# First stage of a two-mixer transformer layer: modulation weights loaded first, x second, two tiles of h modulated from PSUM

## The chip, the cores and the metric

The kernel runs on one core of one Trainium2 chip, in one launch. The metric is device time in microseconds (us) of that launch, taken as the median of several runs; the kernel before was run three times for the numbers below. All data are float32; matmuls that have to be fast take float32 operands split into a high and a low part.

## The reference

x has 2048 rows (tokens) of 1024 columns, c is one vector of 1024. The layer is a modulated token mixer with two kinds of attention, followed by a gated MLP with a short convolution, and a last normalization:

```python
mod = jax.nn.silu(c) @ w_ada[l] + b_ada[l]
shift_a, scale_a, gate_a, shift_m, scale_m, gate_m = [
    m[:, None, :] for m in jnp.split(mod, N_MOD, axis=-1)]

h = rms_norm(x, g_attn[l]) * (1.0 + scale_a) + shift_a
proj = h @ w_in[l]
q_f, k_f, v_f, q_s, k_s, v_s, f_logit = jnp.split(proj, offsets, axis=-1)
...
x = x + gate_a * (mix @ w_out[l])

h = rms_norm(x, g_mlp[l]) * (1.0 + scale_m) + shift_m
...
return rms_norm(x, g_final)
```

Only the first three statements matter here, and of these only the first block of 512 tokens, and the q and k of the first pair of heads of the second attention ("sb", stick-breaking).

## The kernel before

**Tiling.** The tokens are cut into four blocks of 512 (TB), each loaded as four tiles of 128 tokens by 1024 columns. h is kept turned: eight tiles (kt = 0 to 7) of 128 columns by 512 tokens. A unit of attention is a pair of heads of one kind over one block; the first unit is ("sb", 0, 0), and the stage before it is `first_block` (L479).

**What the stage makes.** It needs the columns shift_a and 1 + scale_a (times the gain g_attn) as `mod_a`, 128 partitions by 2 by 8. They come from the first 2048 columns of w_ada, 1024 rows, in four groups g of 256 columns of shift and 256 of scale; group g serves the tiles kt = 2g and 2g + 1. `load_ada(g)` (L173) loads a group with eight DMAs, one for each tile k of 128 rows of w_ada. The class `mod_cols` (L255) sums a group over the 1024 rows in two ways. `add` multiplies row tiles by silu(c) and sums them on DVE (VectorE, L265 and L267) into one tile; DIRECT (L252) says how many of the eight row tiles go this way. `total` (L269) does the rest on PE (TensorE, L275): for each remaining row tile, and once for DVE's partial sum (`None` in the list), four matmuls with a moving operand of a single column. Each float32 matmul shows as two instructions in the profile. `finish` (L277) adds the terms out of the PSUM bank on DVE and puts bias and gain in (L281 to L285).

**What keeps PE at work.** `keep_warm(n)` (L475) issues n matmuls of 256 columns on constants, into a bank that nobody reads. WARM (L251) gives two such numbers and FILL (L252) is the number after every total (L519).

**The rest of the stage.** `normalize_block` (L164) squares and sums a tile of x on ACT (ScalarE, L100), takes the root (L101), the reciprocal on DVE (L102), and scales the tile on DVE (L168). A turn of tile kt is four transposes on PE into one bank (L494); ACT copies the bank to SBUF as `stage` (L495). `stage_h(kt)` (L499) modulates on ACT (L501), splits the result into a high part (ACT, L45) and a low part (DVE, L46), and stores both to DRAM for later units (SP's queue, L505). `project_h(kt)` (L508) is six matmuls (L342), three each for q and k, with the split weights `w[0]`; `w[1](kt)` splits one tile of these weights (L45, L46). `unpack_rows` (L244) turns the small parameter rows (gains, bias) into columns.

**Order.** All loads go out on SP's queue in the order of L215 to L242: c, block 0 of x, the small rows, group 0 of w_ada, half of the raw q and k weights, group 1, the other half, groups 2 and 3, the v weights, block 1 of x. A planner orders the instructions of each engine, from a timeline of its own, except where `fixed()` (L206) ties them: what is traced inside such a block follows, on its engine, whatever the blocks before it issued there. `do(fn, ...)` (L512) is such a block around one call, so that the first stage's order on PE, ACT and DVE is the order of the calls written out. PSUM banks come from pools: `pt` has three, used both by the turns and by the sums of `mod_cols`.

The order of calls before: eight warm-up calls; all four tiles of x normalized; the rows turned and three warm-up calls; all eight turns with their copies; then group 0 is added and totalled, and in a loop over g the sums of group g + 1 are run between the modulations and projections of group g.

Of the kernel before, what the change touches and what calls it, by code (L numbers as in the profile page):

```python
# [9 lines left out]
F32 = mybir.dt.float32  # L10
# [7 lines left out]
P = 128  # L18
# [16 lines left out]
def kernel(ctx: ExitStack, tc: tile.TileContext, x, c, w_ada, b_ada, g_attn, w_in, b_fgate,  # L35
# [125 lines left out]
    def begin_block(tb):  # L161
        blocks.append(load_x(tb))
# [42 lines left out]
    @contextmanager  # L205
    def fixed():  # L206
        with ExitStack() as order:
            for ins in last.values():
                order.enter_context(tc.issue_after(ins))
            n = len(nc.cur_bb.bb.instructions)  # L210
            yield
        for ins in nc.cur_bb.bb.instructions[n:]:
            last[ins.engine] = ins
# [6 lines left out]
        nc.scalar.activation(cs, b[:, :KT], AF.Silu)  # L220
    NR = R_BA + 6 * KT
    rows = sm.tile([NR, P], F32, name="rows")
    begin_block(0)
    for r, src in ((R_GA, g_attn), (R_GM, g_mlp), (R_GF, g_out_fox), (R_GS, g_out_sb), (R_BA, b_ada)):
        n = src.shape[1] // P
        nc.sync.dma_start(rows[r:r + n], src[0].rearrange("(t p) -> t p", p=P))
    load_ada(0)
    raw_qk = load_raw(3 * 512, 4)
    raws = {"qk": next(raw_qk)}
    load_ada(1)  # L230
# [18 lines left out]

    warm = pj()  # L250
    WARM = (8, 3)  # L251
    DIRECT, FILL = 6, 1  # L252
    SPLIT = 4

    class mod_cols:  # L255
# [222 lines left out]

    def first_block(w):  # L479
        xts = blocks[0]  # L480
        with fixed():
            keep_warm(WARM[0])
        for i, xt in enumerate(xts):
            with fixed():
                normalize_block([xt])
        with fixed():
            unpack_rows()
            keep_warm(WARM[1])
        stage = [sb.tile([P, 2, TB], F32, name="xT", tag="K", bufs=5) for _ in range(KT // 2)]
        for kt in range(KT):  # L490
            b = pt()
            with fixed():
                for i, xt in enumerate(xts):
                    nc.tensor.transpose(b[:, i * P:(i + 1) * P], xt[:, kt * P:(kt + 1) * P], ident)  # L494
                nc.scalar.activation(stage[kt // 2][:, kt % 2], b, AF.Copy)  # L495
        aq, ak = pj(), qk()
        hts = []

        def stage_h(kt):  # L499
            hf = px.tile([P, TB], F32, name="hf_a", bufs=2)  # L500
            nc.scalar.activation(hf, stage[kt // 2][:, kt % 2], AF.Identity, scale=mod_a[:, 0, kt:kt + 1],  # L501
                                 bias=mod_a[:, 1, kt:kt + 1])
            h = h_tile()
            split(h[:, 0], h[:, 1], hf, nc.vector)
            nc.sync.dma_start(hs[0][kt], f(h))  # L505
            hts.append(h)

        def project_h(kt):  # L508
            accumulate(aq, 0, w[0], hts[kt], kt)
            accumulate(ak, 1, w[0], hts[kt], kt)  # L510

        def do(fn, *args):  # L512
            with fixed():
# [4 lines left out]
                do(m.total, k)  # L518
                do(keep_warm, FILL)  # L519

        ms = [mod_cols(g) for g in range(KT // 2)] + [None]
        do(ms[0].add, 0, DIRECT)
        do(w[1], 0)
        do(w[1], 1)
        total(ms[0], *range(DIRECT, KT - 1), None, KT - 1)
        for g in range(KT // 2):
            m = ms[g + 1]
            if m:
                do(m.add, 0, 3)
            do(ms[g].finish)  # L530
            if m:
                total(m, *range(DIRECT, KT - 1))
            do(stage_h, 2 * g)
            do(project_h, 2 * g)
            if m:
                do(m.add, 3, DIRECT)
            do(stage_h, 2 * g + 1)
            if m:
                do(w[1], 2 * g + 2)
                do(w[1], 2 * g + 3)  # L540
                total(m, None, KT - 1)
            do(project_h, 2 * g + 1)
        
        with fixed():
            w[1:] = [w[2]()]
        with fixed():
# [1216 lines left out]
```

## Time and profile before

| what | value |
|---|---|
| median of 3 runs | 2947.29 us (2942.23 to 2953.07) |
| the profiled run's own time | 2943.39 us |
| its span on the core | 2941.4 us, 45922 instructions |
| mean granted TensorE clock in it | 0.993 of full speed |
| DMA | 601.89 MB, mean 205 GB/s |

The profile is of one execution. Engines: PE is TensorE's matmuls, PEld its weight loads, DVE VectorE, ACT ScalarE, POOL GpSimd, SP the engine that issues DMAs. A row of the timeline gives start, duration (both us), engine, line, operation, output<-inputs, shapes, how many instructions were merged (x), and in brackets how long the engine was idle before it and what ended that. In a row of a wait, three numbers give the total of us, the times, and the longest. Line 13 of the kernel is L13. A busy PE is not PE at its peak, for the clock that it is granted varies; the views of windows give it as a share of full speed.

### The profile page before, as it was taken

The page shows a single profiled execution, that of the slowest core. Times are in us where ns is not written, and L with a number is a line of the kernel's source. Part 1 is how long each engine was busy: PE and PEld are TensorE (multiplying, and loading weights), DVE is VectorE, ACT ScalarE, POOL GpSimd, SP SyncE. Part 2 cuts the span into 40 slices and gives each one's busy share as a digit, 9 for nine tenths or more (in the row PEclk, how much of TensorE's full clock was granted, in tenths as well). Part 3 has the DMA queues.
Part 4 walks back from the last instruction along what each step waited for, and adds up shares of the span by engine and source line. Part 5 has one row for each costly group of instructions (what it writes and reads, how often), then busy time and mean ns, then how long its engine had stood idle before and what let it go on. Part 6 is the DMA issues. An engine that isn't in the chain of part 4 may idle for free.

```text
span 2941.4 us, 45922 instructions
## 1 busy us (share of the span) xinstructions
PE 2867.8 (97%) x15772; PEld 2459.7 (84%) x15772; DVE 2179.5 (74%) x3464; ACT 1686.0 (57%) x3187; POOL 901.1 (31%) x967
## 2 busy tenths in 40 slices
PE   8999999999999999999999999999999999999998
PEld 7888888888988988888888788888788888888887
DVE  5787778877886656658843788888998888575476
ACT  5776767677776656658744554444444445433342
POOL 0431322243032423231213344444254543142200
PEclk8999999999999999999999999999999999999999
DMA  9749756867469794794537775554754444975644
GB/s 293 255 139 321 236 188 207 301 211 229 162 212 356 269 277 139 232 323 140 182 120 233 245 232 128 130 136 129 236 132 125 130 130 132 309 257 185 216 158 151
DMA packets 348346, 601.89 MB, mean 205 GB/s; under 512 B 34672, under 2 KB 178800, under 8 KB 348112
## 3 DMA queue, kind: packets, MB, share of 16 engines
q1 hardware_dynamic: 324208, 558.06, 57.7%
q0 software_dynamic: 10880, 20.97, 4.3%
q10 hardware_dynamic: 13024, 19.93, 1.9%
q8 instruction: 124, 2.03, 0.3%
q14 instruction: 110, 0.90, 0.1%
HBM read 420.77 MB, written 177.02 MB: 203 GB/s over the span
## 4 chain that ended last, share of the span: by engine, by line
PE 46%; DMA 3%; DVE 2%; SPq 1%; ACT 1%; issue 1%; POOL 0%; DVEq 0%; ACTq 0%; POOLq 0%
PE ps_o L1315 19%; PE ps_t L1315 7%; PE ps_o L1614 6%; PE ps_t L1614 3%; PE ps_bc L1614 3%; PE ps_o L912 1%; PE ps_pv L615 1%; DMA r<-rstd 1%; PE ps_bc L912 1%; PE ps_pt L606 1%; PE ps_o L1609 1%; DMA wo<-wos 1%; DMA hm<-hf_m 1%; SPq L895 1%; DVE op L46 1%
## 5 line engine op out<-in xcount | busy, mean ns | idle before, releaser
L1315 PE MATMUL ps_o<-op,wu 128*128 128x512 f32 x2592 | 608.0, 389 | 2.0 <-DVE snap L1366 1.5
L1315 PEld LDWEIGHTS ps_o<-op,wu 128*128 128x128 f32 x2592 | 486.2, 188 | 103.9 <-DVE snap L1366 1.9
L611 DVE TENSOR_TENSOR at<-ps_pt,at 128x512 fp32r<-128x512 f32 (+1 forms) x576 | 366.1, 652 | 100.2 <-ACT at L610 97.3
L636 DVE TENSOR_TENSOR_SCAN a<-r,a 128x512 f32<-128x512 f32 (+2 forms) x320 | 368.3, 1167 | 77.8 <-ACT a L631 39.9
L342 PE MATMUL ps_pj<-hp,w_qk 128*128 128x512 f32 x1512 | 411.2, 403 | 14.5 <-DMA hp<-hs 12.9
L610 ACT ACTIVATE at<-ps_pt 128x512 fp32r<-128x512 f32 (+1 forms) x576 | 318.5, 576 | 139.1 <-PE ps_pt L606 123.1
L615 PE MATMUL ps_pv<-at,V 128*128 128x256 f32 x2216 | 386.8, 292 | 9.3 <-DVE at L611 4.2
L615 PEld LDWEIGHTS ps_pv<-at,V 128*128 128x128 f32 x2216 | 320.9, 190 | 39.8 <-DVE at L611 11.4
L342 PEld LDWEIGHTS ps_pj<-hp,w_qk 128*128 128x128 f32 x1512 | 275.4, 190 | 71.0 <-DMA hp<-hs 16.2
L45 ACT ACTIVATE wu<-wuraw 128x512 fp32r<-128x512 f32 x204 | 128.9, 632 | 248.5 <-PE ps_o L1315 190.1
L596 PE MATMUL ps_qk<-K,Q 128*128 128x512 f32 (+2 forms) x640 | 265.7, 416 | 5.6 <-ACT a L631 3.3
L413 PE MATMUL ps_pj<-w_v,hp 128*128 128x256 f32 (+1 forms) x1536 | 236.6, 288 | 2.1 <-DVE hp L422 1.6
L597 PE MATMUL ps_qk<-K,Q 128*128 128x512 f32 (+2 forms) x640 | 235.7, 369 | 0.0
L1315 PE MATMUL ps_t<-op,wu 128*128 128x512 f32 x888 | 220.8, 390 | 1.0 <-DVE op L46 1.0
L413 PEld LDWEIGHTS ps_pj<-w_v,hp 128*128 128x128 f32 x1536 | 209.0, 189 | 10.9 <-DVE q L373 1.5
L630 ACT ACTIVATE r<-ps_qk 128x512 f32<-128x512 f32 (+2 forms) x320 | 173.1, 541 | 58.2 <-PE ps_qk L597 55.5
L46 DVE TENSOR_TENSOR wu<-wuraw,wu 128x512 fp32r<-128x512 f32 x204 | 189.6, 930 | 18.1 <-ACT wu L45 16.7
L1315 PEld LDWEIGHTS ps_t<-op,wu 128*128 128x128 f32 x888 | 166.4, 188 | 36.5 <-DVE op L46 1.8
L606 PE MATMUL ps_pt<-edge,a 128*128 128x128 f32 x1088 | 185.1, 274 | 8.4 <-DVE a L636 7.8
L1614 PE MATMUL ps_o<-op 128*128 128x512 f32 x840 | 191.5, 389 | 0.0
L1614 PEld LDWEIGHTS ps_o<-op 128*128 128x128 f32 x840 | 157.7, 188 | 32.7
L679 ACT ACTIVATE p<-p,mn 128x128 f32<-128x128 f32 (+15 forms) x128 | 153.9, 1203 | 53.3 <-DVE mn L675 52.2
(342 smaller groups left out, 5237.6 us busy)
## 6 DMA issues: line engine op xcount, KB each, us to landing
hp<-hs SPq DMA_DIRECT2D x224, 512.0 KB
wuraw<-in_w_up_dram SPq DMA_DIRECT2D x80, 512.0 KB
ra<-g SPq DMA_DIRECT2D x136, 256.0 KB
rb<-in_w_down_dram SPq DMA_DIRECT2D x108, 256.0 KB
g<-u SPq DMA_DIRECT2D x80, 256.0 KB
hs<-hp SPq DMA_DIRECT2D x32, 512.0 KB
hp<-in_w_ada_dram SPq DMA_DIRECT2D x32, 512.0 KB
qk_fox<-q SPq DMA_DIRECT2D x32, 512.0 KB
```

Source lines behind the costliest of these rows:

```text
L46: (lo_engine or nc.gpsimd).tensor_sub(lo, src, f(hi))
L342: nc.tensor.matmul(acc, w[kt][:, a, n], h[:, bb], start=kt == 0 and i == 0, stop=kt == KT - 1 and i == 2)
L413: nc.tensor.matmul(av[:, t * width:(t + 1) * width], hts[kt][:, a, tok], w[1][kt][:, bb, 0:width], start=kt == 0 and m == 0, stop=kt == KT ...
L596: nc.tensor.matmul(b[:, :cw], Q[:, hl, 0, qcols], K[:, hl, :cw], start=True, stop=False)
L597: marks.append(nc.tensor.matmul(b[:, :cw], Q[:, hl, 1, qcols], K[:, hl, :cw], start=False, stop=True).ins)
L606: nc.tensor.transpose(b[:, i * P:(i + 1) * P], blk(kts[kk], qi), ident)
L610: copies = [nc.scalar.activation(at[:, 0, lo:], b[:, lo:], AF.Copy).ins, nc.vector.tensor_sub(at[:, 1, lo:], b[:, lo:], f(at[:, 0, lo:])).ins]
L611: nc.vector.tensor_sub(at[:, 1, lo:], b[:, lo:], f(at[:, 0, lo:])).ins]
L615: m = nc.tensor.matmul(o[:, 0:2 * P], V[kt // 4][:, kt % 4, hl, :], rhs, start=first and kk == 0 and w == 0, stop=last and kk == 1 and w == 1)
L636: nc.vector.tensor_tensor_scan(rev, r[:, 0:need][:, ::-1], rev, 0.0 if right[qi] is None else right[qi][:, 0:1], ALU.mult, ALU.add)
L1315: nc.tensor.matmul(b, w[:, p, j], o[:, q], start=first and i == 0, stop=last and i == 2, skip_group_check=True)
L1614: nc.tensor.matmul(b, a[:, p, t * P:(t + 1) * P], w[:, q], start=first and i == 0, stop=last and i == 2, skip_group_check=True)
```

## The change

The edit moves and reorders work; what is computed stays the same.

- Loads: the eight DMAs of group 0 of w_ada go out ahead of block 0 of x on SP's queue. The five small loads of rows go out on ACT's queue instead of SP's.
- DIRECT is 4 instead of 6, so that each group has five totals on PE (row tiles 4, 5, 6, DVE's partial sum, row tile 7) instead of three, each followed by its warm-up call, and two additions fewer on DVE.
- Group 0 of the modulation is summed and finished ahead of the normalization of x. Three warm-up calls follow each of the four tiles of x, where three calls stood once.
- The tiles kt = 0 and 1 are modulated by ACT straight from the bank into which they are turned. The other six turns and copies are moved into the loop: tiles 2 and 3 ahead of the first projection, tiles 4 to 7 behind the second.
- The sums of group 1 follow those turns; the sums of groups 2 and 3 are spread as before, with the additions cut 2 and 2.

```diff
     NR = R_BA + 6 * KT
     rows = sm.tile([NR, P], F32, name="rows")
-    begin_block(0)
     for r, src in ((R_GA, g_attn), (R_GM, g_mlp), (R_GF, g_out_fox), (R_GS, g_out_sb), (R_BA, b_ada)):
         n = src.shape[1] // P
-        nc.sync.dma_start(rows[r:r + n], src[0].rearrange("(t p) -> t p", p=P))
+        nc.scalar.dma_start(rows[r:r + n], src[0].rearrange("(t p) -> t p", p=P))
     load_ada(0)
+    begin_block(0)
...
-    DIRECT, FILL = 6, 1
+    DIRECT, FILL = 4, 1
...
 
     def first_block(w):
         xts = blocks[0]
-        with fixed():
-            keep_warm(WARM[0])
-        for i, xt in enumerate(xts):
-            with fixed():
-                normalize_block([xt])
-        with fixed():
-            unpack_rows()
-            keep_warm(WARM[1])
-        stage = [sb.tile([P, 2, TB], F32, name="xT", tag="K", bufs=5) for _ in range(KT // 2)]
-        for kt in range(KT):
-            b = pt()
-            with fixed():
-                for i, xt in enumerate(xts):
-                    nc.tensor.transpose(b[:, i * P:(i + 1) * P], xt[:, kt * P:(kt + 1) * P], ident)
-                nc.scalar.activation(stage[kt // 2][:, kt % 2], b, AF.Copy)
+        stage = {}
         aq, ak = pj(), qk()
         hts = []
-
-        def stage_h(kt):
-            hf = px.tile([P, TB], F32, name="hf_a", bufs=2)
-            nc.scalar.activation(hf, stage[kt // 2][:, kt % 2], AF.Identity, scale=mod_a[:, 0, kt:kt + 1],
-                                 bias=mod_a[:, 1, kt:kt + 1])
-            h = h_tile()
-            split(h[:, 0], h[:, 1], hf, nc.vector)
-            nc.sync.dma_start(hs[0][kt], f(h))
-            hts.append(h)
-
-        def project_h(kt):
-            accumulate(aq, 0, w[0], hts[kt], kt)
-            accumulate(ak, 1, w[0], hts[kt], kt)
 
         def do(fn, *args):
             with fixed():
...
                 do(m.total, k)
                 do(keep_warm, FILL)
 
-        ms = [mod_cols(g) for g in range(KT // 2)] + [None]
-        do(ms[0].add, 0, DIRECT)
+        def turn(kt):
+            b = pt()
+            for i, xt in enumerate(xts):
+                nc.tensor.transpose(b[:, i * P:(i + 1) * P], xt[:, kt * P:(kt + 1) * P], ident)
+            return b
+
+        def stage_x(kt):
+            if kt % 2 == 0:
+                stage[kt // 2] = sb.tile([P, 2, TB], F32, name="xT", tag="K", bufs=5)
+            nc.scalar.activation(stage[kt // 2][:, kt % 2], turn(kt), AF.Copy)
+
+        def modulated(kt, src):
+            hf = px.tile([P, TB], F32, name="hf_a", bufs=2)
+            nc.scalar.activation(hf, src, AF.Identity, scale=mod_a[:, 0, kt:kt + 1], bias=mod_a[:, 1, kt:kt + 1])
+            h = h_tile()
+            hts.append(h)
+            nc.scalar.activation(h[:, 0], hf, AF.Copy)
+            return hf, h
+
+        def low(kt, hf, h):
+            nc.vector.tensor_sub(h[:, 1], hf, f(h[:, 0]))
+            nc.sync.dma_start(hs[0][kt], f(h))
+
+        def project_h(kt):
+            accumulate(aq, 0, w[0], hts[kt], kt)
+            accumulate(ak, 1, w[0], hts[kt], kt)
+
+        direct = range(DIRECT, KT - 1)
+        do(keep_warm, WARM[0])
+        m = mod_cols(0)
+        do(m.add, 0, DIRECT)
+        do(unpack_rows)
+        total(m, *direct, None, KT - 1)
+        do(m.finish)
+        for xt in xts:
+            do(normalize_block, [xt])
+            do(keep_warm, WARM[1])
         do(w[1], 0)
         do(w[1], 1)
-        total(ms[0], *range(DIRECT, KT - 1), None, KT - 1)
+        first = []
+        with fixed():
+            first.append(modulated(0, turn(0)))
+            first.append(modulated(1, turn(1)))
         for g in range(KT // 2):
-            m = ms[g + 1]
-            if m:
-                do(m.add, 0, 3)
-            do(ms[g].finish)
-            if m:
-                total(m, *range(DIRECT, KT - 1))
-            do(stage_h, 2 * g)
+            n = mod_cols(g + 1) if g + 1 < KT // 2 else None
+            a = first[0] if g == 0 else None
+            if g:
+                do(m.finish)
+                with fixed():
+                    a = modulated(2 * g, stage[g][:, 0])
+            if n and g:
+                do(n.add, 0, 2)
+            do(low, 2 * g, *a)
+            if g == 0:
+                do(stage_x, 2)
+                do(stage_x, 3)
+            elif n:
+                total(n, *direct)
             do(project_h, 2 * g)
-            if m:
-                do(m.add, 3, DIRECT)
-            do(stage_h, 2 * g + 1)
-            if m:
+            if n and g:
+                do(n.add, 2, DIRECT)
+            if g:
+                with fixed():
+                    a = modulated(2 * g + 1, stage[g][:, 1])
+            else:
+                a = first[1]
+            do(low, 2 * g + 1, *a)
+            if n:
+                if g == 0:
+                    do(n.add, 0, DIRECT)
                 do(w[1], 2 * g + 2)
                 do(w[1], 2 * g + 3)
-                total(m, None, KT - 1)
-            do(project_h, 2 * g + 1)
-        
+                if g == 0:
+                    do(project_h, 1)
+                    for kt in range(4, KT):
+                        do(stage_x, kt)
+                    total(n, *direct)
+                total(n, None, KT - 1)
+            if g:
+                do(project_h, 2 * g + 1)
+            m = n
+
         with fixed():
             w[1:] = [w[2]()]
         with fixed():
```

## The prediction, made before the run

> **What bounds the kernel now.** I read the page first, then the first stage in windows, what ACT waits for there, and TensorE's own timeline. Over the whole run TensorE is the engine that sets the pace:
>
> ```profile
> PE 2867.8 (97%) x15772; PEld 2459.7 (84%) x15772; DVE 2179.5 (74%) x3464; ACT 1686.0 (57%) x3187; POOL 901.1 (31%) x967
> ```
>
> The change touches only the stage before attention, so I look at it in stretches of 20 us (columns: start:end, length, then busy time and instructions of PE, PEld, DVE, ACT, POOL, then the granted clock, DMA share, GB/s):
>
> ```profile
> 20.00:40.00 20.00, 18.10 (x76) 15.66 (x75) 13.04 (x29) 6.78 (x12) 0.00 (x0) 0.66 1.10 338
> ...
> 60.00:80.00 20.00, 18.22 (x131) 16.05 (x130) 13.47 (x22) 14.18 (x33) 5.96 (x8) 1.00 0.81 247
> 80.00:100.00 20.00, 17.43 (x105) 15.07 (x104) 16.83 (x22) 13.60 (x28) 11.27 (x9) 1.00 0.98 336
> ACT hf_a L501 <- DVE mod_a L285: 20.6, 4, 8.3
> ```
>
> From 20 to 40 us PE is busy 18.10 of 20, but its clock is 0.66 of full speed. The last row, of the view of waits, says that ACT stands 20.6 us in total for mod_a, the modulation columns. The timeline tells who makes mod_a late:
>
> ```profile
> 2.51 7.00 PE L477 MATMUL ps_pj<-edge,ones 128*128 128x256 f32 x22
> 10.45 0.25 PE L246 MATMUL ps_pv<-edge,rows 72*128 72x72 f32 x1 [0.93 <-ACT at L100]
> ...
> 13.00 5.05 PE L494 MATMUL ps_pt<-edge,xt 128*128 128x128 f32 x29 [1.04 <-DVE xt L168]
> 18.77 0.68 PE L477 MATMUL ps_pj<-edge,ones 128*128 128x256 f32 x2
> 19.29 0.95 PE L275 MATMUL ps_pt<-ones,adas 128*128 128x1 f32 x8
> ...
> 20.61 0.95 PE L275 MATMUL ps_pt<-cs,ada 128*128 128x1 f32 x8
> 21.42 0.68 PE L477 MATMUL ps_pj<-edge,ones 128*128 128x256 f32 x2
> 24.00 1.84 PE L275 MATMUL ps_pt<-cs,ada 128*128 128x1 f32 x8 [1.90 <-ACT hp L45]
> ...
> 26.34 0.99 PE L342 MATMUL ps_pj<-hp,w_qk 128*128 128x512 f32 x1
> ...
> 29.26 1.70 PE L275 MATMUL ps_pt<-ones,adas 128*128 128x1 f32 x8
> ...
> 31.82 1.71 PE L275 MATMUL ps_pt<-cs,ada 128*128 128x1 f32 x8
> ...
> 38.25 0.58 PE L342 MATMUL ps_pj<-hp,w_qk 128*128 128x512 f32 x1
> ...
> 39.83 0.95 PE L275 MATMUL ps_pt<-ones,adas 128*128 128x1 f32 x8
> ...
> 54.72 0.62 PE L342 MATMUL ps_qk<-hp,w_qk 128*128 128x512 f32 x2
> ```
>
> The reader is to see a PE that works almost without a gap from 24.0 us to the end of the stage at 54.72 + 0.62 = 55.3 us, at two speeds. One row of w_ada summed on PE with its one warm-up call ("a total") takes 20.61 - 19.29 = 1.32 us in the fast part and 31.82 - 29.26 = 2.56 in the slow one; the six matmuls of one projection take 39.83 - 38.25 = 1.58 against 29.26 - 26.34 = 2.92. One warm-up call is two instructions of the first row: 2 x 7.00/22 = 0.64 us. The clock in fine windows of PE alone (length, busy, clock, DMA, GB/s):
>
> ```profile
> 13.20:13.60 0.40, 0.40 (x5) 0.74 0.96 318
> 16.80:17.20 0.40, 0.40 (x5) 0.99 1.17 327
> 23.60:24.00 0.40, 0.00 (x0) 0.54 1.19 309
> 37.20:37.60 0.40, 0.40 (x5) 0.89 1.09 348
> 20.23:23.64 3.41, 1.87 (x13) 1.00 1.10 345
> 1642.12:1645.53 3.41, 1.55 (x7) 1.00 0.98 358
> ```
>
> The clock falls at 13.4, rises at 16.8, falls at 23.6 and rises at 37.3: distances of 3.4, 6.8 and 13.7 us, multiples of one step of 3.41. It spends 13.7 us at half speed after PE ran out of work from 22.1 to 24.0. That loss, about 13.7/2 = 6.8 us of PE work, and the gap of 1.9, is what an order without gaps could win back here.
>
> **The change, part by part.** The times at which one group of mod_a is used, and what the loads and normalization cost:
>
> ```profile
> 22.49 0.81 ACT L501 ACTIVATE hf_a<-xT,mod_a 128x512 f32<-128x512 f32 x1 [3.10 <-DVE mod_a L285]
> 23.87 0.80 ACT L501 ACTIVATE hf_a<-xT,mod_a 128x512 f32<-128x512 f32 x1
> 34.23 0.81 ACT L501 ACTIVATE hf_a<-xT,mod_a 128x512 f32<-128x512 f32 x1 [8.28 <-DVE mod_a L285]
> 42.81 0.81 ACT L501 ACTIVATE hf_a<-xT,mod_a 128x512 f32<-128x512 f32 x1 [5.13 <-DVE mod_a L285]
> 50.39 0.82 ACT L501 ACTIVATE hf_a<-xT,mod_a 128x512 f32<-128x512 f32 x1 [4.12 <-DVE mod_a L285]
> 5.10 1.06 ACT L100 ACTIVATE at<-xt 128x1024 f32<-128x1024 f32 x1 [2.30 <-DMA xt<-in_x_dram]
> 12.19 0.75 DVE L168 TENSOR_SCALAR xt<-xt,ss_a 128x1024 f32<-128x1024 f32 x1
> 13.71 3.90 DVE L267 SCALAR_TENSOR_TENSOR adas<-ada,cs,adas 128x512 f32<-128x512 f32 x5
> 3.10 0.62 SPq L226 DMA_DIRECT2D rows<-in_g_attn_dram  x1
> ...
> 5.09 0.32 SPq L226 DMA_DIRECT2D rows<-in_b_ada_dram  x1
> ada<-in_w_ada_dram SPq DMA_DIRECT2D x32, 256.0 KB
> ```
>
> (a) *Loads.* Eight DMAs of 256 KB, 2.1 MB, now go ahead of x. At the 338 GB/s of the stretch from 20 to 40 us that is 6.2 us, so the last tile of x, scaled at 12.19 + 0.75 = 12.9 us before, is scaled at 19.1. The first 0.5 MB of x was there at 5.10; the first two weight rows now take that place, and the other six follow by 5.1 + 1.57/0.338 = 9.7, early enough for the sums below. The total of bytes ahead of the later groups is the same, so they land when they did. The five small loads of rows leave SP's queue for ACT's, where nothing else is to be done before x arrives; PE needs them at 7.6 us. SP spent 5.09 + 0.32 - 3.10 = 2.3 us on issuing them, while the DMA engines were at work on x, so leaving SP gains nothing that the path sees. Bounds: 0, to +2.3 us should they reach PE late by that much; I take 0. The eight stores of h are issued as before, one per tile, and nothing in this stage reads them.
>
> (b) *PE's opening.* Everything here is in a fixed order: 8 warm-up calls, 2.51 + 8 x 0.64 = 7.6; the turning of rows, 0.25 in the quoted row, 7.9; five totals (rows 4, 5, 6, the partial sum of DVE, row 7, for DIRECT is 4), 5 x 1.32 = 6.6, 14.5; then three warm-up calls after each of the four tiles of x, 12 x 0.64 = 7.6, which wait for nothing: 22.1. Only then comes the first turn of x. On DVE the end of group 0's sums now stands ahead of the scaling of x: it waits for PE's last total, which starts at 7.9 + 4 x 1.32 = 13.2, and is through at 13.2 + 1.88 = 15.1 (the 1.88 is worked out in d); the four scalings behind it, 0.75 and a small reciprocal each, end near 19.1 as well. So x, ready at 19.1, is covered by 3.0 us of warm-up; that cover hides the later x entirely. Were the calls gone, the turn would start at 19.1.
>
> (c) *The two direct tiles.* The next rows price a turn (four transposes), a copy out of the bank, and a modulation that reads a bank, as L569 does:
>
> ```profile
> 70.49 1.47 PE L564 MATMUL ps_pt<-edge,xt 128*128 128x128 f32 x12
> 15.72 0.60 ACT L495 ACTIVATE xT<-ps_pt 128x512 f32<-128x512 f32 x1 [0.25 <-PE ps_pt L494]
> 68.53 1.45 ACT L569 ACTIVATE xm<-ps_pt,mod_a 128x512 f32<-128x512 f32 x2 [5.69 <-PE ps_pt L564]
> 69.94 0.36 PE L596 MATMUL ps_qk<-K,Q 128*128 128x256 f32 x1 [0.74 <-DMA K<-q]
> ```
>
> A turn is 4 x 1.47/12 = 0.5 us. The modulation from a bank, 1.45/2 = 0.73, costs what it does from SBUF (0.81). So the first modulation starts at 22.1 + 0.5 + 0.1 = 22.7, against 22.49: no gain, 0.2 lost. Two copies of 0.60 go from ACT, off the path.
>
> (d) *What is late next.* Six turns that before lay ahead of 18 us now stand behind the first modulation. Turns 2 and 3 need the banks of the first two tiles, the second read until 22.7 + 1.38 + 0.80 = 24.9 (1.38 is 23.87 - 22.49): a new wait in PE's queue, and the first projection stands behind it. Turn 3 ends at 25.5, two projections at 28.7, four turns at the pace of ACT's copies (0.60) about 31.0. Then the sums of group 1: five totals instead of three. The last starts at 31.0 + 4 x 1.32 = 36.3; from the start of the last total to the modulation took 22.49 - 20.61 = 1.88, so group 1 is modulated at 38.2, 3.9 us later than 34.23, and PE is free at 37.6.
>
> (e) *Groups 2 and 3.* Per group PE now does 5 x 1.32 + 2 x 1.58 = 9.8 us. DVE gives up two additions of 3.90/5 = 0.78 per group, and was not the engine that ended the waits. PE: three totals 41.6, projection 43.1, last total starts 44.4, group 2 modulated 46.3 (42.81 before), PE free 45.8; projection 47.4, three totals 51.3, projection 52.9, last total starts 54.2, group 3 modulated at 56.1 against 50.39. From there the two last projections ended 55.3 - 50.39 = 4.9 us later, so the stage ends at 61.0.
>
> *Sum:* 61.0 - 55.3 = +5.7 us. Taken apart: eight more totals (20 instead of 12, 10.6) and nine more warm-up calls (20 instead of 11, 5.8) in PE's stream, less the half-speed loss (6.8); the remaining 3.9 is gaps that the denser stream closes, 1.9 of them the one from 22.1. Behind the stage PE has work waiting in order, busy 18.22 of the 20 us from 60, so I carry the 5.7 through whole. The profiled run took 2943.4 us (a span of 2941.4 and 2.0 around it): 2949.1. The median of the three runs shown lies 3.9 above that run, so the forecast for a median is 2953.0.
>
> *The clock, weighed.* The sum needs full speed through stretches that hold only totals, where warm-up fills 0.68 of every 1.32 us, 51%. No such window was seen at full speed. Bounds from the quoted windows: 20.23:23.64 was followed by a fall though it was busy 1.87 of 3.41; but only some 1.2 us of that, 36%, were warm-up calls, the rest matmuls of a single column, so I read it that these do not count. 1642.12:1645.53, busy 1.55 (45%) with wide matmuls, was followed by no fall. The 51% lie above the kept window, so I take "holds" at no cost; "falls" is the second case. The Trainium skill, "TensorE: Matmul & The Clock Gate", Part 1, has the clock halved only after an idle window of about 3.4 us; here 1.9 us of idleness sufficed, so the trace disagrees, and the second case below keeps its chance. Its Part 4 says that transposes do not count as busy to that gate; by that rule the stretch from 22.1 to 25.5 would count as idle and cost one more half-speed stretch, 6.8 us, to 2959.8, which the second case takes in. The trace disagrees again: transposes alone (L494) filled 13.4 to 16.8, and the clock rose at the end.
>
> **The rivals.** *Half clock (slower).* In the stretch of totals from 31.0 to 41.6 the clock falls and, as from 23.6 to 37.3, a lone projection does not raise it. For it: totals and short projections stayed at half for 13.7 us before. Against it: 45% was enough elsewhere. Price: between one more such stretch, +6.8, and all of 37.6 to 61.0 at half, +23.4; with the 5.7, 2960 to 2976, taken at 2966. It decides where the share of warm-up in a window falls below what keeps the gate open.
>
> *Absorbed (not slower).* The first attention matmul waited for K at 69.94, and PE is idle 20 - 18.22 = 1.8 and 20 - 17.43 = 2.6 us in the two stretches to 100 us. If these waits are on transfers that a later first stage does not delay, 4.4 of the 5.7 are taken up: +1.3, 2948.6. Against it: PE was busy 18.22 of 20 us around K's arrival, with work that a later stage shifts whole.
>
> *Order elsewhere.* Only the first stage's order is fixed; the rest is planned anew around it. PE's idle time, 2941.4 - 2867.8 = 73.6 us, could shift by a third, 25 us, either way: 2928 or 2978. Nothing in the profile speaks for a sign.
>
> **How the numbers follow.** Forecast 0.48 (its own range 2949 to 2959: up by the 2.3 us of (a) and by two steps at half speed, 3.4; down by the 3.9 between profiled run and median), half clock 0.27, absorbed 0.15, order 0.10. The range runs from 2940 to 2974, which leaves out the ends of the second and fourth case. About 0.5%, 14.7 us, is what a measurement of this kernel can tell from no change. Slower by more: 0.23 of half clock, 0.05 of order, 0.02 of the forecast, 0.30. Faster by more: 0.05 of order, 0.02 of absorbed, 0.07. Within: 0.63.
>
> **What would show it.** Right: twelve warm-up calls between the last total of group 0 and the first turn, no PE gap before 22 us, modulations near 22.7, 38, 46 and 56 us, the last projection ending near 61, and a clock of 1.0 from 17 to 61. Wrong: a half clock in the totals (second rival); the first turn waiting for x beyond 22 us, which would mean that the loads cost more than (a); totals below 1.3 us; or an end of the stage near 61 with attention's first matmul still at 70 (third).

## The result, and the profile after

The changed kernel took 2967.88 us (median of five runs, 2965.64 to 2979.19) against 2948.97 us before: a ratio of 1.0074, 95% interval 1.0059 to 1.0088. It is slower by more than the 0.5% that a measurement of this kernel can tell. The profiled execution took 2967.88 us with a span of 2966.2, 24.8 us longer than the span of before, 2941.4. The execution of before that was profiled took 2943.39 us, 5.6 below its median, so the two profiles lie further apart than the two medians (18.9 us).

The busy times of the whole run (the first part of the page), and then the first stage in stretches of 20 us (start:end, length, busy time and instructions of PE, PEld, DVE, ACT, POOL, then the granted clock, DMA share and GB/s), of the changed kernel:

```profile
PE 2887.4 (97%) x15870; PEld 2477.5 (84%) x15870; DVE 2172.4 (73%) x3456; ACT 1686.0 (57%) x3185; POOL 902.5 (30%) x967
```

```profile
20.00:40.00 20.00, 19.15 (x117) 16.96 (x116) 10.34 (x22) 9.61 (x19) 0.00 (x0) 0.87 1.09 336
40.00:60.00 20.00, 19.69 (x108) 17.02 (x107) 6.82 (x19) 5.54 (x9) 0.00 (x0) 0.87 0.86 287
60.00:80.00 20.00, 18.13 (x136) 16.99 (x136) 11.62 (x35) 13.57 (x38) 0.17 (x1) 1.00 0.56 159
```

PE is busy 19.6 us more than before (2867.8) and idle 5.2 more: 2966.2 - 2887.4 = 78.8 against 73.6. From 20 to 60 us it hardly stands still, as the prediction wanted, but its clock is 0.87, not 1.00. The same stage on PE's timeline (start, length, then the instructions; the wait before a row in brackets):

```profile
2.74 6.05 PE L477 MATMUL ps_pj<-edge,ones 128*128 128x256 f32 x16
...
14.04 0.95 PE L275 MATMUL ps_pt<-cs,ada 128*128 128x1 f32 x8
14.85 5.86 PE L477 MATMUL ps_pj<-edge,ones 128*128 128x256 f32 x26
20.55 1.47 PE L497 MATMUL ps_pt<-edge,xt 128*128 128x128 f32 x12
22.35 0.66 PE L497 MATMUL ps_pt<-edge,xt 128*128 128x128 f32 x4 [0.32 <-ACT hf_a L507]
23.53 0.50 PE L342 MATMUL ps_pj<-hp,w_qk 128*128 128x512 f32 x1 [0.53 <-ACT hp L510]
...
28.45 1.05 PE L275 MATMUL ps_pt<-cs,ada 128*128 128x1 f32 x8
29.36 0.68 PE L477 MATMUL ps_pj<-edge,ones 128*128 128x256 f32 x2
29.88 0.95 PE L275 MATMUL ps_pt<-cs,ada 128*128 128x1 f32 x8
...
33.85 0.95 PE L275 MATMUL ps_pt<-cs,ada 128*128 128x1 f32 x8
34.66 1.08 PE L477 MATMUL ps_pj<-edge,ones 128*128 128x256 f32 x2
35.53 1.71 PE L275 MATMUL ps_pt<-cs,ada 128*128 128x1 f32 x8
...
38.09 1.71 PE L275 MATMUL ps_pt<-cs,ada 128*128 128x1 f32 x8
...
62.16 0.62 PE L342 MATMUL ps_qk<-hp,w_qk 128*128 128x512 f32 x2
```

From 28.45 us there is nothing on PE but totals; at about 34.7 their matmuls go from 0.95 to 1.71 us, and a total from 1.32 to 38.09 - 35.53 = 2.56. The stage ends at 62.16 + 0.62 = 62.8 us, against 55.3 before and 61.0 in the forecast. The clock around that point, in windows of PE alone (length, busy, clock, DMA, GB/s), and the modulations on ACT:

```profile
31.07:34.48 3.41, 3.41 (x29) 1.00 1.10 349
...
34.50:34.90 0.40, 0.40 (x4) 0.88 1.10 348
34.66:45.00 10.34, 10.34 (x39) 0.51 0.85 257
...
45.00:45.40 0.40, 0.40 (x3) 0.95 1.07 440
```

```profile
12.61 1.06 ACT L100 ACTIVATE at<-xt 128x1024 f32<-128x1024 f32 x1 [9.40 <-DMA xt<-in_x_dram]
...
21.52 1.45 ACT L507 ACTIVATE hf_a<-ps_pt,mod_a 128x512 f32<-128x512 f32 x2 [1.44 <-PE ps_pt L497]
...
35.57 0.81 ACT L507 ACTIVATE hf_a<-xT,mod_a 128x512 f32<-128x512 f32 x1 [6.20 <-DVE mod_a L285]
...
48.43 0.82 ACT L507 ACTIVATE hf_a<-xT,mod_a 128x512 f32<-128x512 f32 x1 [9.40 <-DVE mod_a L285]
...
57.83 0.81 ACT L507 ACTIVATE hf_a<-xT,mod_a 128x512 f32<-128x512 f32 x1 [5.94 <-DVE mod_a L285]
```

PE was busy 3.41 of the 3.41 us before the fall, so idleness did not drop the clock. It stayed at half for 10.24 us, three steps of 3.41. Group 0 is modulated 1.0 us sooner than before (22.49), group 1 1.3 us later (34.23), groups 2 and 3 by 5.6 and 7.4 (42.81, 50.39): the part at half speed lies between.

### The profile page after: what moved, and what is told of

The parts are those of the page before. It is cut to its first block, busy times and chain, and to the rows that moved or that the text cites. A ratio compares the mean times of both kernels' runs of the same rounds, so it can differ in the third digit from the quotient of the medians.

```text
span 2966.2 us, 46096 instructions
## 1 busy us (share of the span) xinstructions
PE 2887.4 (97%) x15870; PEld 2477.5 (84%) x15870; DVE 2172.4 (73%) x3456; ACT 1686.0 (57%) x3185; POOL 902.5 (30%) x967
## 4 chain that ended last, share of the span: by engine, by line
PE 45%; DMA 2%; DVE 2%; SPq 1%; issue 0%; ACT 0%; POOL 0%; DVEq 0%; ACTq 0%; POOLq 0%
PE ps_o L1347 19%; PE ps_t L1347 7%; PE ps_o L1646 6%; PE ps_t L1646 3%; PE ps_bc L1646 3%; PE ps_o L944 2%; PE ps_bc L944 1%; DMA r<-rstd 1%; PE ps_o L1641 1%; SPq L927 0%; PE ps_pv L647 0%; DMA hm<-hf_m 0%; PE ps_pt L638 0%; DMA x1s<-x1u 0%; PE ps_bc L1641 0%
## 5 line engine op out<-in xcount | busy, mean ns | idle before, releaser
L413 PEld LDWEIGHTS ps_pj<-w_v,hp 128*128 128x128 f32 x1536 | 210.6, 190 | 12.2 <-issue 2.5
L46 DVE TENSOR_TENSOR wu<-wuraw,wu 128x512 fp32r<-128x512 f32 x204 | 188.2, 923 | 18.5 <-ACT wu L45 17.3
```

Of the source, the lines that this page charges most:

```text
L46: (lo_engine or nc.gpsimd).tensor_sub(lo, src, f(hi))
L413: nc.tensor.matmul(av[:, t * width:(t + 1) * width], hts[kt][:, a, tok], w[1][kt][:, bb, 0:width], start=kt == 0 and m == 0, stop=kt == KT ...
```

## The experiments

All were timed beside the kernel before, in three sessions, each on its own chip; the medians of before there were 2947.37 (E1 to E4), 2947.38 (F1 to F4) and 2949.33 us (G1 to G4). Two more numbers serve for each kernel. *Clock loss* is the span times one minus the granted clock, the mean over its runs: what half speed would have cost if PE never stood still (the clock is given to 0.001, so one run is good to some 1.5 us). *Rest* is the mean time less that loss. For the kernel before, the clock loss was 26.2, 26.2 and 26.1 us, the rest 2921.7, 2921.2 and 2922.2, so that both bear comparison across sessions.

| kernel | median us (runs) | ratio, 95% interval | stage end us | clock loss | rest |
|---|---|---|---|---|---|
| before (E session) | 2947.37 (32) | 1 | 55.3 | 26.2 | 2921.7 |
| changed, first runs | 2967.88 (5) | 1.0074 (1.0059 to 1.0088) | 62.8 | 31.5 | 2938.8 |
| F1 changed again | 2973.19 (6) | 1.0086 (1.0070 to 1.0103) | 68.9 | 35.2 | 2937.5 |
| E1 before, 17 calls more | 2963.51 (9) | 1.0042 (1.0028 to 1.0056) | 62.7 | 28.0 | 2934.6 |
| E2 before, loads of the change | 2956.44 (12) | 1.0025 (1.0013 to 1.0037) | 63.5 | 29.6 | 2927.0 |
| E3 changed, DIRECT 6 | 2953.43 (12) | 1.0014 (1.0001 to 1.0027) | 58.8 | 27.1 | 2926.6 |
| E4 changed, FILL 2 | 2961.40 (12) | 1.0043 (1.0030 to 1.0056) | 65.6 | 17.8 | 2942.9 |
| F2 changed, FILL 2 in group 1 | 2964.66 (6) | 1.0060 (1.0043 to 1.0076) | 60.4 | 27.7 | 2937.1 |
| F3 changed, x first | 2979.09 (5) | 1.0113 (1.0095 to 1.0131) | 80.2 | 40.5 | 2939.0 |
| F4 before, gap filled | 2944.95 (12) | 0.9992 (0.9981 to 1.0003) | 57.2 | 22.8 | 2921.9 |
| G1 before, DIRECT 4 | 2966.63 (6) | 1.0064 (1.0048 to 1.0079) | 64.7 | 36.6 | 2930.3 |
| G2 before, DIRECT 7 | 2949.41 (12) | 1.0004 (0.9992 to 1.0016) | 57.8 | 29.0 | 2920.4 |
| G3 changed, no warm-ups | 2964.12 (6) | 1.0059 (1.0041 to 1.0077) | 65.3 | 38.0 | 2926.7 |
| G4 before, DIRECT 7, gap filled | 2952.37 (12) | 1.0011 (0.9999 to 1.0023) | 58.8 | 27.3 | 2924.1 |

The stage end is that of the one profiled execution. It varies from run to run: the changed kernel itself ended the stage at 62.8 us in one and at 68.9 in the other.

**E1, a later end of the stage.** Ahead of the sum of all DVE rows of group 3:

```
             if m:
                 do(w[1], 2 * g + 2)
                 do(w[1], 2 * g + 3)
+                if g == 2:
+                    do(keep_warm, 17)
                 total(m, None, KT - 1)
```

> The kernel before, with 17 more warm-up calls on PE ahead of the last two totals of group 3, and nothing else: a pure delay of the end of the first stage by 17 x 0.45 = 7.65 us, at full clock (0.45 us a call is what 13 calls in a row took in the changed kernel, 5.86/13). Theory A (carried once): the stage ends near 63 us instead of 55.3 and the kernel takes +7 to +9 us (+0.25 to +0.3%), so that the other 12 us or so of the change come from something else in it. Theory B (a later stage meets the waits and the clock's windows behind it differently, whatever made it late): +15 to +25 us (+0.5 to +0.85%), as the change.

The stage ended at 62.7 us, as the changed kernel's, and the mean time (clock loss and rest together) rose from 2947.9 to 2962.6, by 14.7 us: twice the 7.4 of the delay. So a stage that ends later by 7.4 us costs more than 7.4. But E1 is not a delay alone: the planner also made another order of the work behind the stage, much as it did in the changed kernel (see *Behind the stage*). The changed kernel's mean over its eleven runs, 2971.5, is 23.6 above that of before; E1 has some three fifths of that.

**E2, the loads alone.** The rows go on ACT's queue and `load_ada(0)` ahead of `begin_block(0)` in the kernel before.

> The kernel before with the loads of the change alone (group 0 of w_ada ahead of x, rows on ACT's queue). x is scaled last near 20.4 us instead of 12.9, so the turns end near 25.5 and the first modulation comes near 30 instead of 22.5; but group 1's weights are there by then, so the gap of 1.9 us and the 13.7 us at half clock may go. If the loads by themselves are what costs, the stage ends 7 or more later (62 or more) and the kernel takes +7 us or more. If their cost is given back in the gap and the clock, it ends at 54 to 58 and the kernel takes -2 to +4 us.

PE's first turns in E2 wait for x, one after the other:

```profile
16.00 0.47 PE L494 MATMUL ps_pt<-edge,xt 128*128 128x128 f32 x1 [6.30 <-DVE xt L168]
17.36 0.47 PE L494 MATMUL ps_pt<-edge,xt 128*128 128x128 f32 x1 [0.89 <-DVE xt L168]
```

The loads alone cost 9.1 us of the median in the order of before, with a first modulation at 29.68 us instead of 22.49. **F3** undoes them in the changed kernel:

```
     rows = sm.tile([NR, P], F32, name="rows")
+    begin_block(0)
...
-        nc.scalar.dma_start(rows[r:r + n], ...)
+        nc.sync.dma_start(rows[r:r + n], ...)
     load_ada(0)
-    begin_block(0)
```

> The changed kernel with the loads in the order of the kernel before (x and the rows ahead of the modulation weights, on the same queue). Theory (in the changed order TensorE's calls end just as x is ready, so the later x costs little, and the weights first are what the order needs): the totals of group 0 wait for their weights until about 17 us, the first turn comes near 24 us, the stage ends 3 to 5 us later than 62.8, time 2968 to 2974 us. Rival (the loads are what costs): first turn ahead of 20 us, stage end 59 to 61 us, time 2 to 4 us under the changed kernel's.

The first total of group 0 in F3, on PE's timeline, waits for its weights, and the first turn comes late:

```profile
14.56 1.86 PE L275 MATMUL ps_pt<-cs,ada 128*128 128x1 f32 x8 [3.93 <-DMA ada<-in_w_ada_dram]
...
34.99 2.13 PE L497 MATMUL ps_pt<-edge,xt 128*128 128x128 f32 x16
```

I had put the first turn near 24 us; it came at 34.99, since the clock fell in the waits of PE's opening, and the five totals, at 2.56 us each, and most of the warm-ups behind them ran at half. The order of PE's opening needs the weights first; the loads are not what is wrong with the change.

**E3 and G1, the number of totals.** In the changed kernel `DIRECT, FILL = 6, 1`; in the kernel before `DIRECT, FILL = 4, 1`.

> The changed kernel with DIRECT back at 6: three totals a group instead of five. Theory of the totals: groups 1 to 3 lose 6 x 1.32 = 7.9 us of PE, and the stretch of totals alone is shorter, so the clock may hold; the stage ends at 50 to 55 instead of 62.8, and the kernel takes 8 to 20 us less than the changed one (2948 to 2960). If the stage's end is set by DVE's additions or the weights' landing instead, it ends near 60 and gains 3 us or less.

> The kernel before with DIRECT 4 alone: eight more totals on TensorE, two fewer additions per group on DVE; loads, order and warm-ups as before. Theory (the greater part of the changed kernel's loss is the work of these totals, 8 x 1.32 = 10.6 us at full clock and more at half): stage end 64 to 69 us against 55.3, time 2957 to 2964 us, ratio 1.0035 to 1.0055, that is over half of the way from the kernel before to the changed one. Rival (the totals only fill time in which TensorE waited for DVE's sums, and the order of loads and turns is what costs): stage end 55 to 60 us, time 2946 to 2952 us.

E3 ended its stage at 58.8 us, where 50 to 55 was expected, though its time lies in the range given. G1 ended its stage at 64.7, within the 64 to 69 of the theory, and its time lies 2.6 us above the theory's range. The two agree from both sides on the totals, each taken with the order that the planner then makes of the rest. The change without its eight extra totals is 1.0014; the eight totals without the rest of the change are 1.0064. In G1 the rest rises by 2930.3 - 2922.2 = 8.1 us, near the 8 x 1.32 = 10.6 of their work, and the clock loss by 36.6 - 26.1 = 10.5. The gap of 1.9 us on PE is closed there, and still the clock falls, now at 27.0, for 13.7 us. G1's PE from 20 to 40 us (length, busy, clock, DMA, GB/s):

```profile
20.00:40.00 20.00, 20.00 (x96) 0.67 1.10 341
```

A PE that is never idle and a clock of 0.67, where before it was 18.10 busy and 0.66.

**E4 and F2, more warm-up among the totals.** E4 sets FILL to 2. F2 does so in group 1 alone:

```
         def total(m, *ks):
             for k in ks:
                 do(m.total, k)
-                do(keep_warm, FILL)
+                do(keep_warm, FILL + (m.g == 1))
```

> The changed kernel with two warm-up calls after every total (FILL 2). If the clock fell at 34.5 us because totals with one call fill too little of a window, it now holds at 1.0 from 17 us to the end of the stage; each of the 15 later totals takes 1.77 instead of 1.32 us (+6.8), the opening 2.2 more, the half clock gives 5.1 back: the stage ends near 66. If it fell for another reason (a gap, the transposes), it falls again near 34 to 38 us and the stage ends at 70 or later.

> The changed kernel with a second warm-up call per total in group 1 alone, the one whose totals stand alone on TensorE from 28.45 us. Theory (the clock fell at 34.5 us because five totals in a row with one call each do not hold it): no fall before 45 us in most executions, five more calls of 0.45 us, stage end 57.7 + 2.3 = 60.0 us against 62.8, time 2 to 3 us under that of the changed kernel in this call. Rival (groups 2 and 3 do not hold the clock either, the fall only moves on): a half-clock stretch between 38 and 58 us, stage end 63 to 65 us, time as the changed kernel's or above.

PE's timeline of F2 in group 1, and its clock:

```profile
30.71 0.95 PE L275 MATMUL ps_pt<-cs,ada 128*128 128x1 f32 x8
31.52 1.11 PE L477 MATMUL ps_pj<-edge,ones 128*128 128x256 f32 x4
32.47 0.95 PE L275 MATMUL ps_pt<-cs,ada 128*128 128x1 f32 x8
```

```profile
20.00:40.00 20.00, 19.15 (x129) 1.00 1.09 335
40.00:60.00 20.00, 19.69 (x120) 1.00 0.86 298
```

With two calls a total takes 32.47 - 30.71 = 1.76 us, 0.44 more, and the clock stays at 1.00 through the stage. It ends at 60.4, as the theory said (60.0). The time is 8.5 us under F1's, of which 35.2 - 27.7 = 7.5 is clock loss. E4 holds the clock as well (no window of its first stage is below 1.00) and has by far the least clock loss, 17.8 us, but its twenty more calls are work: the stage ends at 65.6 us and the rest goes to 2942.9. So wide work among the totals, meaning matmuls of more than one column, decides whether the clock holds in the first stage of the executions profiled here; and more calls, which hold it, do not bring the kernel back to the time of before.

**F1, the changed kernel again**, for the runs to be compared with on one chip.

> The changed kernel once more, beside the kernels of this call. Theory (the changed order costs more than the later stage end alone): median 2965 to 2970 us, ratio 1.006 to 1.008; time less the time lost to a lower clock (span x (1 - granted clock), mean over the runs) again near 2939 us against 2922 of the kernel before. Rival (the five runs taken so far fell on many half-clock stretches by chance, and the change costs what a pure delay of the stage by 7.4 us costs): near 2963 us, ratio about 1.005, and time less clock loss near 2935 us.

The median, 2973.19, lies above what both theories expected. The rest is 2937.5 (2938.8 in the first runs), nearer to the 2939 of the first than to the 2935 of the second, which is little to choose by. The clock loss is higher still, 35.2, which may come of where the windows of the clock happen to lie. In F1's profile the clock fell in the first five totals too (PE's windows):

```profile
9.41:12.82 3.41, 3.41 (x28) 1.00 0.98 352
12.60:13.00 0.40, 0.40 (x5) 0.78 1.03 420
```

The 26 warm-up instructions behind them then ran in part at half speed, and the first turn came at 23.40 us instead of 20.55.

**G3, no warm-ups between totals and turn:** `WARM = (8, 0)` in the changed kernel.

> The changed kernel without the twelve warm-up calls between the totals of group 0 and the first turn. Theory (the calls end just with x, so they cover nothing by their length and serve the clock alone): the first turn still comes at 20 to 21 us, TensorE is idle from 14.9 until then, the clock falls near 17 to 20 us and stays at half until the projections are through, 3.4 to 6.8 us lost, time 3 to 7 us above the changed kernel's, 2971 to 2980 us. Rival (the calls, not x, set the first turn): first turn 2 us or more earlier, time the same or lower.

```profile
17.06 0.69 PE L497 MATMUL ps_pt<-edge,xt 128*128 128x128 f32 x2 [0.54 <-DVE xt L168]
17.92 0.69 PE L497 MATMUL ps_pt<-edge,xt 128*128 128x128 f32 x2 [0.17 <-DVE xt L168]
...
19.77 2.46 PE L497 MATMUL ps_pt<-edge,xt 128*128 128x128 f32 x10 [0.30 <-DVE xt L168]
```

The rival was right. On PE's timeline the first turn begins tile by tile at 17.06, as DVE scales them. The clock fell already at 13.75, among the totals and ahead of where the calls would stand, so not from the idleness that I had expected. The clock loss is up by 2.8 on F1's, but the rest fell by 10.8 us. Some 5.4 of that are the calls themselves, 12 x 0.45; the remainder I can't place. G3's interval overlaps those of the changed kernel, so a gain without the calls isn't shown; that they gained nothing is.

**F4, G2, G4, the other direction.** F4 puts `do(keep_warm, 4)` behind the totals of group 0 in the kernel before; G2 sets DIRECT to 7 there; G4 does both.

> The kernel before with four warm-up calls, 1.8 us, behind the totals of group 0, where TensorE stood idle from 22.1 to 24.0 us and the clock fell at 23.6. Theory (that gap is what dropped the clock, and a half-clock stretch in the first stage is paid in full): no fall at 23.6, up to 6.8 us back, stage end 49 to 52 us against 55.3, time 2940 to 2944 us, ratio 0.997 to 0.999. Rival (the clock falls a window later in the totals, or the stretches behind the stage take it back): stage end 53 to 56 us, time 2945 to 2949 us.

> The kernel before with DIRECT 7: four totals fewer, one more addition of 0.78 us per group on DVE. Theory (TensorE's work of totals sets the pace of this stage): 4 x 1.32 = 5.3 us less, stage end 49 to 53 us, time 2940 to 2944 us. Rival (with that DVE's sums come last and TensorE waits for them): waits of TensorE on adas in the first stage, stage end 54 to 58 us, time 2946 to 2951 us.

> The kernel before with DIRECT 7 and with the four warm-up calls behind the totals of group 0. Theory (both gains add: fewer totals, and no gap that drops the clock): 2937 to 2942 us, ratio 0.9965 to 0.9985. Rival (TensorE waits for DVE's sums, and the calls only lengthen it): 2946 to 2951 us.

F4's interval reaches 1.0003, so it can't be told from the kernel before, and its stage ended at 57.2, later than both expectations; in its profile the clock fell at another place, in a wait of 1.83 us for w_ada ahead of the first total. Filling one gap is not enough when another wait opens a window. In G2 PE's waits in the first 66 us (in total, times, longest) show why four totals fewer bring nothing:

```profile
PE ps_pt L275 <- DVE adas L267: 5.6, 4, 1.9
PE ps_pj L342 <- ACT hp L45: 3.3, 1, 3.3
```

The 5.3 us of work saved came back as 5.6 us of waiting for DVE's sums (0.5 before). With DIRECT 6, then, taking totals off PE only makes it wait for DVE. G4 came out at 2952.37 us, with 4.4 us of such waits in its first 66 us, above the 2937 to 2942 of its theory and its rival's range too: the two gains do not add. None of the twelve experiments beat both kernels beyond doubt.

## Where the prediction was right and where it was wrong, step by step

The time lay inside the range, but the likeliest case, no change that can be told, did not happen. The half-clock rival, 0.27, was right on what the clock does and where: in the totals from 31.0 us, seen at 34.7. That its time, 2960 to 2976 and taken at 2966, fits as well is luck. It put the whole loss into the first stage, 6.8 to 23.4 us on top of an end at 61.0; in the profiled run that stage ended at 62.8, its stretch at half speed cost 10.24/2 = 5.1 us, and most of the time was lost behind the stage, of which the rival says nothing.

**(a) Loads: nearly right.** The last tile of x was scaled at 19.70 + 0.75 = 20.45 us against 19.1. ACT waited 9.40 us for the first of x. The rows came in time: PE turned them without a wait.

**(b) PE's opening: right in time, wrong in its cover.** The first turn came at 20.55, not 22.1. A warm-up call was taken at 0.64 us from the row of 22 instructions in 7.00 us, but part of that row ran at half speed. At full speed 26 instructions took 5.86 us, so a call is 0.45. The twelve calls therefore ended 0.1 us behind x in place of 3.0, and in F1, partly at half speed, 3 us later. G3 shows that a turn can begin before the last tile of x is there: the calls stood in its way.

**(c) Direct tiles: right.** The first modulation came 0.97 us behind the start of the first turn (0.6 forecast), at 21.52 against 22.49 before; its 1.0 us of gain comes from (b).

**(d) Late next: right in mechanism.** Turn 2 waited 0.32 us for the bank, as named, and the five totals of group 1 stood behind all turns. Group 1 was modulated at 35.57, not 38.2, since all that stood ahead of it, the calls first, ended sooner; the clock fell only behind its last total.

**(e) Groups 2 and 3: 48.43 and 57.83 against 46.3 and 56.1.** Here the totals at 2.56 us bite. The stage ended 7.4 us later than before in place of 5.7.

**The sum: what was missed lies behind the stage.** The forecast took +10.6 (totals) + 5.8 (calls) - 6.8 (half speed won back) - 3.9 (gaps closed), and nothing behind the stage. For the gaps, PE in the first 66 us and behind (length, busy, clock, DMA, GB/s), kernel before and then changed:

```profile
0.00:66.00 66.00, 57.55 (x307) 0.87 0.96 309
66.00:2990.00 2924.00, 2810.23 (x15468) 1.00 0.62 199
```

```profile
0.00:66.00 66.00, 61.84 (x346) 0.92 0.90 294
66.00:2990.00 2924.00, 2825.52 (x15524) 0.99 0.63 199
```

Idle in the first 66 us was 8.45 us and is 4.16: -4.3, as forecast. Behind it PE's idle time went from 2941.4 - 66 - 2810.23 = 65.2 to 2966.2 - 66 - 2825.52 = 74.7, +9.5. By the granted clock of the two profiles, the stretches at half speed add up to 17.1 us in the first stage and 23.3 behind it before, and to 10.2 and 43.7 after. Half of each is lost: 3.4 us less in the first stage, and 10.2 more behind it.

| term | forecast us | measured us |
|---|---|---|
| eight totals with their calls, 8 x 1.32 at full speed | +10.6 | +10.6 |
| nine more calls | +5.8 | +4.1 (9 x 0.45) |
| clock in the first stage | -6.8 | -3.4 |
| clock behind it | 0 | +10.2 |
| idle in the first stage | -3.9 | -4.3 |
| idle behind it | 0 | +9.5 |
| sum | +5.7 | +26.7, of the 24.8 of the two spans |

Two steps failed. The one that cost most is "so I carry the 5.7 through whole": the stage ended 62.8 - 61.0 = 1.8 us behind the forecast, but the span came out 24.8 - 5.7 = 19.1 us above it; behind the stage a delay of 7.4 us grew to 24.8. The other is *The 51% lie above the kept window, so I take "holds" at no cost*: the fall cost 5.1 us in the profiled run. F1's first stage spent 23.9 us at half speed, a cost of 12.0.

F2 tells the two apart. Its first stage is about what the forecast drew, an end at 60.4 us for 61.0 and a clock of 1.00 from the totals on. Yet it took 2964.66 - 2947.38 = 17.3 us more than the kernel before, where 5.7 were forecast: 11.6 us for the first step that failed. The 8.5 us by which F1 lies above F2 hold the price of the second, but not it alone: F1 also has an order of work far behind the stage that F2 has not (see below).

The profile of before is a favourable execution. Its 23.3 us at half speed behind the stage are the least of all fourteen profiles, the others having 27.4 to 44.5, so some of the 10.2 us belongs to that one execution. Over all runs the clock loss of the changed kernel is 33.5 us in the mean of its eleven runs against 26.2, +7.3 where -6.8 was forecast, and the rest is up by some 16.4 where 10.6 + 5.8 - 3.9 = 12.5 was.

The 51% itself was worked out wrongly. 0.68 is the length that a row of two pipelined instructions is drawn with. From one row's start to the next a total takes 1.32 us and its call 29.88 - 29.36 = 0.52 of it, 39%, which is below the 45% of the window that the prediction trusted. F2 has what the prediction thought it had: 32.47 - 31.52 = 0.95 of 1.76, 54%, and its clock held.

**Behind the stage.** The same PE instruction, looked up in two traces, tells how late a kernel is against the kernel before at that place. Places are given by the time in the kernel before, and each value is the median over a few us. The planner orders what lies behind the first stage anew in each kernel, and it changed PE's order at two places: between 66 and 107 us, and between some 2100 and 2165 us.

| kernel | late at 60 us | at 118 | at 2060 | from 2200 on | new order at 66 to 107 | new order at 2100 to 2165 |
|---|---|---|---|---|---|---|
| changed | 7.4 | 10.2 | 20.9 | 24.7 | yes | yes |
| F1 | 13.5 | 16.2 | 22.8 | 27.0 | yes | yes |
| E1 | 7.4 | 10.1 | 22.1 | 24.7 | yes | yes |
| G1 | 9.4 | 12.2 | 16.4 | 20.4 | yes | yes |
| E4 | 10.2 | 13.0 | 9.3 | 12.9 | yes | yes |
| E3 | 3.4 | 6.2 | 11.4 | 10.6 | yes | no |
| F2 | 5.0 | 7.8 | 17.5 | 17.4 | yes | no |
| E2 | 8.2 | 8.2 | 10.2 | 13.6 | no | yes |
| F4 | 1.9 | 1.9 | -0.2 | -1.0 | no | no |

Where the first place has the new order, the delay grows there by 2.7 to 2.8 us, however late the kernel came (3.7 in G3); with the order of before it grows by 0.0 to 0.8 (E2, F4, G2). Where the second place has a new order, it grows by 2.6 to 4.2 us (F3, G2 and G3 too); without one it does not grow (G4 too). Rows of PE at the first place, of the kernel before, the changed kernel and E2:

```profile
97.14 2.80 PE L413 MATMUL ps_pj<-w_v,hp 128*128 128x264 f32 x21 [0.93 <-DVE hp L422]
105.81 4.33 PE L413 MATMUL ps_pj<-w_v,hp 128*128 128x264 f32 x21 [2.35 <-DVE hp L422]
105.33 2.81 PE L413 MATMUL ps_pj<-w_v,hp 128*128 128x264 f32 x21 [0.93 <-DVE hp L422]
```

In the new order PE waits longer for hp, and the 21 matmuls behind the wait run in part at half speed; E2, about as late but in the old order, has neither. So *Order elsewhere* had a part: 2.8 + 3.9 = 6.7 of the 17.3 us by which the changed kernel's delay grew. No run changes these orders alone, so this rests on the other kernels' profiles, one of each, agreeing. It also touches what the experiments tell: E1 and G1 carry both new orders, E3 and F2 are without the second, so each shows its edit together with what the planner made of it. The other 10.6 us come in between the two places. There the changed kernel has 13.6 us more at half speed, which is 6.8 of them; F1, the same kernel, has 6.5 us between the places in all, and E4 falls back by 3.7. What decides where those stretches fall stays open. The *absorbed* rival, +1.3 us, is excluded: by 118 us no kernel's delay had shrunk.

## What to carry to other kernels

Before work is moved onto TensorE to close its gaps, work out what share of a window its wide matmuls fill, from the starts of the rows and not from their lengths: single-column matmuls keep the engine busy and still let its clock fall. Work that another engine does in time (here DVE's additions) is not free on TensorE, and taking it off again brings nothing once the two are in balance. And where a planner orders the rest, compare its orders before and after the edit far behind it, too: two places that nobody touched go with 6.7 us of this loss.

## What the runs showed of the hardware

**A busy TensorE is slowed down.** From the starts of the rows I worked out, in each step of 3.41 us of the first stage, the share that is not single-column matmuls and not idle, and set it beside what the clock did next:

| kernel, window (us) | clock in it | share of wide work | clock next |
|---|---|---|---|
| changed 31.39:34.80 | full | 34% | half |
| F1 9.41:12.82 | full | 35% | half |
| G1 23.58:26.99 | full | 39% | half |
| G1 20.16:23.58 | full | 42% | full |
| changed 10.90:14.31 | full | 45% | full |
| F1 33.31:36.73 | full | 45% | half |
| changed 48.46:51.87 | full | 53% | full |
| before 27.06:30.47 | half | 64% | half |
| F1 46.97:50.38 | half | 74% | full |
| changed 41.63:45.04 | half | 83% | full |

In the first stage of all fourteen profiles the clock, once full and past the opening, fell behind every window below 40% and behind none above 50%; between them both happened. To rise again took more: behind windows of up to 66% it did not, from 86% on it always did, and from 74 to 84% both happened. Totals with one call each lie on that edge: a window holds two calls or three, by where it begins, which fits that the same kernel spent 10.2 us of its first stage at half speed in one execution and 23.9 in another. The Trainium skill, "TensorE: Matmul & The Clock Gate", Part 1, says that the window is 3.4 us long and free-running, which every step here bears out; that an idle window is what lowers the clock, these rows contradict.

**The start is at half speed though the clock's column says 1.00.** In the changed kernel the opening warm-ups number 6 in the 2.00 us from 2.80, and 11 in the same length later (PE's windows):

```profile
2.80:4.80 2.00, 2.00 (x6) 1.00 0.91 297
...
16.00:18.00 2.00, 2.00 (x11) 1.00 1.15 326
```

The column seems to know only changes of the clock; a cost per instruction taken from an opening is too high.
